# Sample scores as four 32-column products, sample values for two heads in turn, and the schedule repeated with latest times as ranks

## The chip, the cores and the metric

The kernel runs on one core of one Trainium2 chip. The metric is the device time of one execution in microseconds (us), from the start to the end of the program on that core, as a median of several runs. A profile of one execution shows the five engines: PE (TensorE, the matrix multiplier; its weight loads are listed apart as PEld), DVE (VectorE), ACT (ScalarE), POOL (GpSimd) and SP (SyncE, which here only issues transfers), and the DMA traffic. "Granted clock" is the share of full speed at which the throttle let TensorE run.

## The reference

One layer of a hybrid encoder. The input is a prompt of 2048 tokens and a "sample" of 8 sequences of 16 tokens (together 128 rows), each of width 1024. One input projection feeds three groups of heads: 6 forgetting-attention heads (FoX), 6 RWKV-7 heads and 4 heads that attend to 256 memory tokens. All heads are 64 wide. Their gated outputs go through one output projection and are added to the input. Cut to what the change touches, the sample's attention is:

```python
def fox_attend_block(q, cq, qpos, k, v, ck, kpos):
    s = jnp.einsum('bqhd,bkhd->bhqk', q, k, preferred_element_type=jnp.float32) * (HEAD_DIM ** -0.5)
    s = s + jnp.transpose(cq, (0, 2, 1))[..., :, None] - jnp.transpose(ck, (0, 2, 1))[..., None, :]
    mask = kpos[None, :] <= qpos[:, None]
    s = jnp.where(mask, s, jnp.finfo(jnp.float32).min)
    p = jax.nn.softmax(s, axis=-1)
    return jnp.einsum('bhqk,bkhd->bqhd', p.astype(v.dtype), v)

def fox_sample(q, k, v, logf, k_past, v_past, logf_past):
    keys = jnp.concatenate([k_past.astype(k.dtype), k], axis=1)      # 512 cached keys + 16 own, per sequence
    vals = jnp.concatenate([v_past.astype(v.dtype), v], axis=1)
    ...
def mem_attend(q_cols, mem_q_g, mk, mv):                             # the same without decay, 256 keys
    ...
```

Each of the 8 sequences has its own cached keys and values, so nothing is shared between sequences: a query row of sequence s may only meet the keys of sequence s.

## The kernel before, in words

**Two stages.** The first stage (lines 160 to 925) projects the input and runs the RWKV heads. The projection's products are named `pjd` and `pjt` (and `ptok`, `psh`); they stream 512 or 256 columns and depend on little. The RWKV work comes in blocks of 512 tokens for a pair of heads, twelve in all for the prompt. A block is a long chain of small products with work of the other engines between them: `gw`, `gx` (line 460 on), `pvt`/`pat`, `pmv`, `pbt` (turns and small triangular parts), `pz`, `pa`, `sc`, `sy` (the scan, eight dependent steps of `sc`), `yc`, `pss`, `spr` (the group norm). Small products use a quarter (64x64) or a sixteenth (32x32) of the array, so that several lie in it side by side. The second stage (line 926 on) does the attention and the output projection: for each key block `pm` (a running maximum over the keys), `pS` (scores, three products in the parts that a split number has), `P`, `Ph`, `Pl` (exponential on ACT, its split on ACT and POOL), `po` (values), and `py` (the output projection), which fills gaps.

**The sample** (function `sample`, lines 1189 to 1284) runs in the second stage, in five steps of two heads each: three FoX pairs with 512 keys and two memory pairs with 256. Per pair `load` brings the queries (`sC`), and then for each head in turn: `masked` takes a buffer `sD`, clears its first 640 columns on POOL (line 1219) and copies the queries into it (line 1222), and loads the cached values (`sA`, line 1226) and keys (`sB`, line 1229), 1 MB each for FoX and 0.5 MB each for memory. The 128 rows of the contraction hold the 64 dimensions of one sequence above those of another, so one product serves two sequences; the queries lie in a 128-column operand whose other columns are zero, and four such products (sequence pairs 0 to 3) add up in one bank `pS3` (the page shows it as `pS<-sB,sD`). `soft` is the softmax on DVE and ACT, with `pN` for the sample's own 16 keys. `turn` transposes the weights (`pt3b`). `values` multiplies them with `sA`: 8 sequences x 4 blocks of keys, each a product of a 64-column operand with 16 columns (`po<-sD,sA`), into the upper or lower half of the bank `po3` by head. A product in plain fp32 shows as two passes in the trace, so these 32 products are 64 passes.

**Buffers.** `sA`, `sB`, `sC`, `sD`, the output weights and some others share seven buffers of 8 KB per partition (`big`, line 965, `BIG` is 7), handed out in the order of the program.

**The order of the work.** The body of the kernel only records instructions. At the end `_arrange` (line 1849) sorts them anew for every engine: `_schedule` (line 1702) is a list scheduler with a model of each instruction's length, of TensorE's clock and of the buffers; at each step it takes the instruction that can start first, and among those that can start equally early the one with the smallest rank. A rank is the instruction's place in the recorded program, in time, less a weight times the longest chain that hangs on it. Four weights and two settings of a preference for staying in the array's present shape (`_WEIGHTS`, `_STAY`) are tried, and the order with the shortest modelled time is kept. SP's transfers are part of it and start in that order too: a transfer that waits for a buffer holds up those behind it.

Of the kernel before, what the change touches and what calls it, by code (L numbers as in the profile page):

```python
# [16 lines left out]
D = 1024  # L17
# [34 lines left out]
def kernel(ctx: ExitStack, tc: tile.TileContext, I: dict, O: dict):  # L52
# [24 lines left out]
    pools = _Pools(tc)  # L77
# [848 lines left out]
    with ExitStack() as p2:  # L926
# [261 lines left out]
        def sample(fox, hp):  # L1188
# [26 lines left out]
            def masked(h):  # L1215
                rr = slice(64 * h, 64 * h + 64)
                R["D"] = big("sD")
                qm = R["qm"] = R["D"][:, 0:640]
                G.memset(qm, 0.0)
# [11 lines left out]
            def soft(h):  # L1231
                hh, rr = 2 * hp + h, slice(64 * h, 64 * h + 64)
                pS = qb_.tile([128, 512], F32, tag="pm", name="pS3", bufs=PMB)
                for sp in range(4):
                    mm(pS[:, :nk], R["qm"][:, 128 * sp:128 * sp + 128], R["ck"][:, sp], start=sp == 0, stop=sp == 3)
                sb = R["sb"] = R["D"][:, 640:1280]
                st = wk.tile([128, 4], F32, tag="st3", name="st3")
                if fox:
# [3 lines left out]
                    dg = R["D"][:, 1920:2048]  # L1242
# [14 lines left out]
            def turn(h):  # L1257
                PT = R["PT"] = R["D"][:, 1280:1920].rearrange("p (a b) -> p a b", b=128)
# [194 lines left out]
_WEIGHTS = (0.0, 0.15, 0.3, 0.45)  # L1453
_STAY = (0, 2500)
# [247 lines left out]
def _schedule(prog, runs, over, weight, stay, loose=(), rank=None):  # L1702

    ins, eng, cost, deps, tiles, tile = prog
    nodes, node = runs
    count = len(nodes)
    of = [eng[m[0]] for m in nodes]
    before = [sorted({node[j] for k in m for j in deps[k]} - {x}) for x, m in enumerate(nodes)]  # L1710
    used = [sorted({n for k in m for n in tiles[k]}) for m in nodes]
    seen = lambda a, b: (0 if a == "PE" else 15) if a == b != "SP" else _SEEN[b]
    succ, soft, need = [[] for _ in nodes], [[] for _ in nodes], [len(d) for d in before]
    pool = {n: t.mls.memorylocations[0].ant_tile_pool_name for n, t in tile.items()}
    first, queue, uses, left, free_at = {}, {}, {}, {}, {}
    for x in range(count):
        for j in before[x]:
            succ[j].append(x)
        for n in used[x]:
            uses[n] = uses.get(n, 0) + 1  # L1720
            left[pool[n]] = left.get(pool[n], 0) + 1
            if n not in first:
                first[n] = x
                queue.setdefault(tile[n].tag, []).append(n)
                free_at[tile[n].tag] = [0] * tile[n].tag_meta.bufs
            elif first[n] not in before[x]:
                soft[first[n]].append(x)
                need[x] += 1
# [16 lines left out]
    for x in range(count - 1, -1, -1):  # L1745
# [3 lines left out]
        for q in after[x]:  # L1749
            gate[q] = max(gate.get(q, 0), below[x])  # L1750
# [222 lines left out]
```

## Time and profile before

| what | value |
|---|---|
| median of 3 runs | 1887.29 us (1883.79 to 1889.1) |
| time of the profiled execution | 1892.18 us |
| its span, first to last instruction | 1890.1 us |
| mean granted clock | 0.954 |
| PE busy | 1784.7 us (94%) |
| DVE, ACT, POOL busy | 949.0, 874.9, 788.9 us (50%, 46%, 42%) |
| sample's score products, FoX | 48 passes, 26.6 us busy |
| sample's value products | 512 passes, 34.4 us busy |
| read from and written to HBM | 211.47 and 87.12 MB |

"Busy" is the time in which at least one instruction of the engine was under way; matmuls overlap each other, so the time from one start to the next is shorter than the duration of one. In answers of the time line, a row is "start, length, engine, line, operation, out<-in, sizes of the operands, count"; a row of several passes runs from the first start to the last end. In answers by stretch ("windows"), each engine has its busy time and, in brackets, its number of instructions, then come the granted clock (PEclk), the share of DMA time and the GB/s. A pass that streams 512 columns shows 128x512, and 128*32 ahead of it would be the operand that stays in the array (rows x columns).

### The profile page before, as it was taken

The numbers are of one execution on the slowest core, as the hardware profiler recorded it, in microseconds if no ns is written. First come the engines' busy times: TensorE is split into PE (matmuls) and PEld (weight loads), VectorE is DVE, ScalarE is ACT, GpSimd is POOL, SyncE is SP. The second block draws the span as 40 slices with busy tenths as digits, with TensorE's granted clock in tenths as the row PEclk, the third lists the DMA queues.
The fourth block names the chain that finished last, engine by engine and source line by source line (L and its number), as shares of the span: only waits on it lengthen the run. The fifth ranks groups of instructions, "written<-read, shape, count | busy, mean of one in ns | idle before, by whom it ended". The sixth has DMA issues, their size and how long they took to land. (4 is left out here: it accounts for less than half of the span.)

```text
span 1890.1 us, 42104 instructions
## 1 busy us (share of the span) xinstructions
PE 1784.7 (94%) x16743; PEld 1426.4 (75%) x16743; DVE 949.0 (50%) x2330; ACT 874.9 (46%) x1727; POOL 788.9 (42%) x790
## 2 busy tenths in 40 slices
PE   5979999899999999998999997899898999999998
PEld 4878988688887888776788886666665666667776
DVE  6544444464444563453744543767445544386213
ACT  5424342424234323324232424687687555876452
POOL 5564342142132232121321331377485443866463
PEclk9989999999999999998999896799999889999999
DMA  7665455535436555354455344435546644254332
GB/s 245 228 227 169 153 175 182 191 123 176 163 117 207 177 167 196 109 176 163 127 164 188 103 155 123 141 126 167 188 137 209 186 139 137 67 179 145 137 114 100
DMA packets 213274, 301.34 MB, mean 159 GB/s; under 512 B 57444, under 2 KB 162454, under 8 KB 197206
## 3 DMA queue, kind: packets, MB, share of 16 engines
q1 hardware_dynamic: 213078, 298.66, 48.2%
q8 instruction: 131, 2.15, 0.5%
q14 instruction: 65, 0.53, 0.1%
HBM read 211.47 MB, written 87.12 MB: 158 GB/s over the span
## 5 line engine op out<-in xcount | busy, mean ns | idle before, releaser
L59 PE MATMUL pjd<-xk,w 128*128 128x512 f32 (+5 forms) x2280 | 526.4, 375 | 18.9 <-ACT qk L705 6.7
L59 PEld LDWEIGHTS pjd<-xk,w 128*128 128x128 f32 (+1 forms) x2280 | 385.8, 191 | 87.4 <-issue 9.5
L62 POOL TENSOR_TENSOR Pl<-P,Ph 128x512 fp32r<-128x512 f32 (+3 forms) x272 | 315.5, 1170 | 165.5 <-ACT Ph L1120 144.7
L59 PE MATMUL pjt<-w,xk 128*128 128x256 f32 x2040 | 290.3, 291 | 6.7 <-POOL w L62 4.2
L59 PEld LDWEIGHTS pjt<-w,xk 128*128 128x128 f32 x2040 | 266.2, 194 | 17.8 <-issue 5.0
L59 PE MATMUL py<-W,oh 128*128 128x512 f32 x816 | 247.1, 403 | 1.9 <-DVE rb L1162 0.9
L1117 ACT ACTIVATE P<-pS,NB 128x512 f32<-128x512 f32 x240 | 148.5, 623 | 110.9 <-PE pS L59 85.0
L59 PEld LDWEIGHTS py<-W,oh 128*128 128x128 f32 x816 | 150.9, 190 | 39.7 <-DVE rb L1162 1.4
L59 PE MATMUL pS<-Q,K 128*128 128x512 f32 (+2 forms) x480 | 160.1, 400 | 4.5 <-ACT P L1117 4.0
L59 PE MATMUL po<-Ph,vt 128*65 128x512 f32 x480 | 158.3, 381 | 0.3 <-ACT ob L1143 0.2
L1120 ACT CAST Ph<-P 128x512 fp32r<-128x512 f32 (+3 forms) x272 | 151.4, 564 | 9.2 <-PE po L59 4.0
L59 PEld LDWEIGHTS pS<-Q,K 128*128 128x128 f32 (+1 forms) x480 | 89.1, 198 | 36.6 <-ACT P L1117 16.0
L62 DVE TENSOR_TENSOR xo<-py,xo 128x512 f32<-128x512 f32 x68 | 46.8, 689 | 133.2 <-PE py L59 133.0
L1063 DVE CUSTOM_DVE_ANT_0 jk<-pm,nb,mx 128x512 bf16<-128x512 f32 (+3 forms) x144 | 93.0, 646 | 30.6 <-PE pm L59 22.8
L62 POOL TENSOR_TENSOR nr<-nr,mhalf 128x8 f32<-128x8 f32 (+2 forms) x43 | 61.5, 1431 | 97.5 <-DVE nr L68 73.0
L59 PE MATMUL pm<-K,Q 128*128 128x512 f32 (+2 forms) x240 | 96.4, 415 | 5.7 <-DVE mx L1063 4.8
L62 POOL TENSOR_TENSOR w<-wraw,w 128x1024 fp32r<-128x1024 f32 (+1 forms) x34 | 80.7, 2375 | 44.3 <-ACT w L197 43.2
L59 PE MATMUL po<-Pl,vt 128*65 128x512 f32 x240 | 91.1, 380 | 0.6 <-POOL Pl L62 0.6
L59 PEld LDWEIGHTS po<-Ph,vt 128*65 128x65 f32 x480 | 65.2, 141 | 26.6 <-issue 2.2
L705 ACT COPY qk<-pjt 128x512 f32<-128x512 f32 (+1 forms) x47 | 26.5, 563 | 113.1 <-PE pjt L59 92.0
L1063 DVE CUSTOM_DVE_ANT_0 jk<-pm,nb 128x512 bf16<-128x512 f32 (+3 forms) x96 | 61.3, 638 | 33.0 <-PE pm L59 28.3
L62 POOL TENSOR_TENSOR oh<-ot,oh 128x384 fp32r<-128x384 f32 (+2 forms) x38 | 45.2, 1191 | 57.0 <-ACT oh L1321 32.0
(392 smaller groups left out, 2942.6 us busy)
## 6 DMA issues: line engine op xcount, KB each, us to landing
w<-w_d SPq DMA_DIRECT2D x84, 1024.0 KB
w_d<-w SPq DMA_DIRECT2D x28, 1024.0 KB
y_d<-xo SPq DMA_DIRECT2D x21, 512.0 KB
wraw<-in_w_in SPq DMA_DIRECT2D x36, 256.0 KB
xo<-in_x SPq DMA_DIRECT2D x17, 512.0 KB
xo<-y_d SPq DMA_DIRECT2D x17, 512.0 KB
xt<-in_x SPq DMA_DIRECT2D x24, 256.0 KB
xraw<-in_xT SPq DMA_DIRECT2D x24, 256.0 KB
```

What stands on the lines that cost most here:

```text
L59: PE.matmul(out, lhsT, rhs, start=start, stop=stop, skip_group_check=True)
L62: e.tensor_tensor(out=out, in0=a, in1=b, op=op)
L705: S.copy(o_, out)
L1063: V.tensor_tensor_reduce(out=jk[:, :n], in0=pm[:, :n], in1=U["nb"][:, h, c0:c0 + n], scale=1.0, scalar=-3.0e38 if c0 == 0 else m_, op0=A_, ...
L1117: S.activation(P_[:, c0:], pS[:, c0:], AF.Exp, bias=NB[:, qb, 2 * hp + h, kt:kt + 1] if fox else 0.0)
L1120: S.copy(Ph[:, c0:], P_[:, c0:])
```

## The change

The change has three parts.

- **Scores.** The zero-padded operand shrinks from 640 to 128 columns, with the queries of sequence pair `sp` in columns 32sp to 32sp+31. The four products per head now have 32 columns each, go into four different 32-row strips of the bank, and no longer add up.
- **Values.** `values` is called once per pair instead of once per head, and issues the two heads' products in turn: upper half of the bank, lower half, upper half. The final scaling is one DVE instruction over 128 rows instead of two over 64. Both heads' `sD` and `sA` are now held until then.
- **The order.** `_schedule` also returns for each instruction the latest time at which it could start without making the modelled total longer. The planner runs five rounds from each of three weights (0.3, 0.45, 0.6); after each round the ranks move by 0.4 towards these latest times, and the shortest of the fifteen modelled orders is kept. The preference for staying in a shape is no longer tried.

```diff
             def masked(h):
                 rr = slice(64 * h, 64 * h + 64)
-                R["D"] = big("sD")
-                qm = R["qm"] = R["D"][:, 0:640]
+                D = R["D", h] = big("sD")
+                qm = R["qm"] = D[:, 0:128]
                 G.memset(qm, 0.0)
...
-                    V.tensor_copy(qm[64 * j:64 * j + 64].rearrange("p (s c) -> p s c", c=160)[:, :, 16 * j:16 * j + 16],
+                    V.tensor_copy(qm[64 * j:64 * j + 64].rearrange("p (s c) -> p s c", c=32)[:, :, 16 * j:16 * j + 16],
                                   q3[:, :, j, :])
                 m = big("sA")[:, 0:512 * nkt]
-                R["cv"] = m.rearrange("p (s t d) -> p s t d", t=nkt, d=64)
+                R["cv", h] = m.rearrange("p (s t d) -> p s t d", t=nkt, d=64)
...
                 for sp in range(4):
-                    mm(pS[:, :nk], R["qm"][:, 128 * sp:128 * sp + 128], R["ck"][:, sp], start=sp == 0, stop=sp == 3)
+                    mm(pS[32 * sp:32 * sp + 32, :nk], R["qm"][:, 32 * sp:32 * sp + 32], R["ck"][:, sp])
...
-            def values(h):
-                rr = slice(64 * h, 64 * h + 64)
+            def values():
                 po = qa.tile([128, 512], F32, tag="pt", bufs=PTB, name="po3")
+                rows = [slice(0, 64), slice(64, 128)]
                 if fox:
-                    mm(po[rr, 0:128], R["vn"][:, rr], R["PT"][:, 4, :], stop=False)
+                    for h, rr in enumerate(rows):
+                        mm(po[rr, 0:128], R["vn"][:, rr], R["PT", h][:, 4, :], stop=False)
                 for s_ in range(8):
                     for t in range(nkt):
-                        mm(po[rr, 16 * s_:16 * s_ + 16], R["cv"][:, s_, t, :], R["PT"][:, t, 16 * s_:16 * s_ + 16],
-                           start=not fox and t == 0, stop=t == nkt - 1)
-                stt(R["gt"][rr], po[rr, 0:128], 0.5, R["gt"][rr], M, M)
+                        for h, rr in enumerate(rows):
+                            mm(po[rr, 16 * s_:16 * s_ + 16], R["cv", h][:, s_, t, :], R["PT", h][:, t, 16 * s_:16 * s_ + 16],
+                               start=not fox and t == 0, stop=t == nkt - 1)
+                stt(R["gt"], po[:, 0:128], 0.5, R["gt"], M, M)
...
-                r += [lambda f=f, h=h: f(h) for f in (masked, soft, turn, values)]
-            return r + [out]
+                r += [lambda f=f, h=h: f(h) for f in (masked, soft, turn)]
+            return r + [values, out]
...
-_WEIGHTS = (0.0, 0.15, 0.3, 0.45)
-_STAY = (0, 2500)
+_TRIES = ((0.3, 0), (0.45, 0), (0.6, 0))
+_AGAIN = 5
+_SHIFT = 0.4
...
+    total = max(end)
+    late = [total - (end[x] - start[x]) for x in range(count)]
+    for x in reversed(order):
+        e = of[x]
+        for j in p.before[x]:
+            late[j] = min(late[j], late[x] - (1 if of[j] == e == "PE" else end[j] - start[j] + p.seen(of[j], e)))
+        for j, at in why[x]:
+            late[j] = min(late[j], late[x] - (at - start[j]))
+    return total, start, late
...
-    _, _, start = min((_schedule(prog, runs, over, w, stay, _LOOSE) for w in _WEIGHTS for stay in _STAY),
-                      key=lambda x: x[0])
+    found = []
+    for w, stay in _TRIES:
+        rank = p.emitted(w)
+        for _ in range(_AGAIN):
+            total, start, late = _schedule(p, rank, stay, _LOOSE)
+            rank = [(1 - _SHIFT) * a + _SHIFT * b for a, b in zip(rank, late)]
+            found.append((total, start))
+    _, start = min(found, key=lambda x: x[0])
```

The list `why` holds, for an instruction that took over a buffer, the instruction that had released it. The rest of the diff makes a class of what `_schedule` computed at its start.

The new order moves instructions everywhere. Three places follow. The first is PE in the last RWKV block of the first stage, the end of its chain; `pt<-ident,tok` are turns of keys for the second stage, `pjd` are products of the input projection. Before:

```order
L983 MATMUL pt<-ident,tok 128x128 x4
L59 MATMUL pmv<-su,gm 64x64 x16
L59 MATMUL pbt<-ident,bk 64x64 x32
L59 MATMUL pz<-su,XT_120 64x128 x16
L983 MATMUL pt<-ident,tok 128x128 x4
L59 MATMUL sc<-su,bt 64x64 x16
L59 MATMUL sy<-gm,su 64x64 x16
L59 MATMUL pa<-bt,za 64x64 x16
L59 MATMUL pa<-gm,za 64x64 x16
L983 MATMUL pt<-ident,tok 128x128 x6
L59 MATMUL sc<-ST,AD 128x64
L59 MATMUL sc<-st,AD 128x64 x3
```

Now, in the same place of that block:

```order
L59 MATMUL pbt<-ident,bk 64x64 x31
L59 MATMUL pjd<-xk,w 128x512 x6
L59 MATMUL pz<-su,XT_120 64x128 x16
L59 MATMUL pjd<-xk,w 128x512 x8
L59 MATMUL pa<-bt,za 64x64 x16
L59 MATMUL pa<-gm,za 64x64 x16
L59 MATMUL sc<-su,bt 64x64 x16
L59 MATMUL sy<-gm,su 64x64 x16
L59 MATMUL sc<-ST,AD 128x64
L59 MATMUL pjd<-xk,w 128x512 x3
L59 MATMUL sc<-st,AD 128x64
```

Before, the projection was finished ahead of this block, and 22 turns of keys stand in it; now 48 `pjt` and 39 `pjd` products of the projection stand between its steps, and the turns of keys come after it.

The second place is PE at the first sample pair (`pS_17445` and `pS_17630` are the scores of head 0 and head 1 of the pair before, `po_17500` the values of head 0). Before:

```order
L1263 MATMUL pt3b<-ident,sD 128x128
L59 MATMUL po_17500<-sD,sC 64x128
L59 MATMUL po_17500<-sD,sA 64x16 x32
L59 MATMUL pm<-K_16178,Q_17599 128x512
L59 MATMUL pS_17630<-sB,sD 128x512
L59 MATMUL pS<-Q_17197,K_16179 128x512 x2
L59 MATMUL pS_17630<-sB,sD 128x512
L59 MATMUL pS<-Q_17195,K_16177 128x512
L59 MATMUL pS<-Q_17197,K_16179 128x512
```

Now (`pS_17445` and `pS_17578` are the two heads' scores; the pair's values, `po_17668<-sD,sA 64x16 x64`, come 20 rows further on):

```order
L59 MATMUL pS_17445<-sB,sD 32x512 x4
L59 MATMUL pN_17452<-sC 128x128
L59 MATMUL pN_17452<-sD,one_82 128x128
L983 MATMUL pt<-ident,tok 128x128 x2
L59 MATMUL pm<-K_16177,Q_17563 128x512
L983 MATMUL pt<-ident,tok 128x128 x2
L1263 MATMUL pt3b<-ident,sD 128x128 x5
L59 MATMUL pS_17578<-sB,sD 32x512 x4
```

The second head's scores no longer wait behind the first head's values, and a head's four score products stand together, where attention products stood between them before.

The third place is SP, where the cached values and keys of a FoX pair are fetched. Before (the last FoX pair):

```order
L1226 DMA sA<-in_cfv 128x2048
L1229 DMA sB<-in_cfkT 128x2048
L1146 DMA sd<-rs 1x512
L1170 DMA rc<-sd 32x32
L1226 DMA sA<-in_cfv 128x2048
L1279 DMA o_d<-sC 128x128
L1173 DMA rd<-rc 32x32
L1176 DMA rb_18100<-rd 64x512 x2
L1229 DMA sB<-in_cfkT 128x2048
```

Now:

```order
L1226 DMA sA<-in_cfv 128x2048
L1281 DMA o_d<-sC 128x128
L1229 DMA sB<-in_cfkT 128x2048
L1226 DMA sA<-in_cfv 128x2048
L1146 DMA sd<-rs 1x512
L988 DMA vtok<-v_d 128x4x128
L1229 DMA sB<-in_cfkT 128x2048
```

The output of the pair before (`o_d<-sC`) now leaves between the first two of the four loads, so all four stand behind the values of the pair before; previously the first head's two loads stood ahead of them.

More of the change, by code (lines that the diff above doesn't have):

```diff
@@ L1699, in run @@
         return s, s + (own - c.own) + c.time + (w - 1) * c.own
[L1702 to L1728, printed above, removed]
-    after = [sorted({q for n in used[x] for q in over.get(pool[n], ())}) for x in range(count)]
-    pooled, below, at, own = {}, [0] * count, 0, [0] * count
-    def length(m, e):
-        c = [cost[k] for k in m]
@@ new lines, with __init__, seen, length @@
+class _Problem:
+    def __init__(self, prog, runs, over):
+        self.ins, self.eng, self.cost, deps, tiles, self.tile = prog
+        self.nodes, node = runs
+        nodes, tile = self.nodes, self.tile
+        self.count = count = len(nodes)
+        self.of = of = [self.eng[m[0]] for m in nodes]
+        self.before = before = [sorted({node[j] for k in m for j in deps[k]} - {x}) for x, m in enumerate(nodes)]
+        self.used = used = [sorted({n for k in m for n in tiles[k]}) for m in nodes]
+        self.succ, self.soft, self.need = [[] for _ in nodes], [[] for _ in nodes], [len(d) for d in before]
+        self.pool = pool = {n: t.mls.memorylocations[0].ant_tile_pool_name for n, t in tile.items()}
+        self.queue, self.uses, self.left, first = {}, {}, {}, {}
+        for x in range(count):
+            for j in before[x]:
+                self.succ[j].append(x)
+            for n in used[x]:
+                self.uses[n] = self.uses.get(n, 0) + 1
+                self.left[pool[n]] = self.left.get(pool[n], 0) + 1
+                if n not in first:
+                    first[n] = x
+                    self.queue.setdefault(tile[n].tag, []).append(n)
+                elif first[n] not in before[x]:
+                    self.soft[first[n]].append(x)
+                    self.need[x] += 1
+        self.after = [sorted({q for n in used[x] for q in over.get(pool[n], ())}) for x in range(count)]
+        self.spent = [self.length([self.cost[k] for k in m], e) for m, e in zip(nodes, of)]
+        self.below, gate = [0] * count, {}
+        for x in range(count - 1, -1, -1):
+            tail = 150 if of[x] == "PE" else 0
+            self.below[x] = self.spent[x] + max([self.below[s] + self.seen(of[x], of[s]) + tail for s in self.succ[x]] +
+                                                [gate.get(pool[n], 0) for n in used[x]], default=0)
+            for q in self.after[x]:
+                gate[q] = max(gate.get(q, 0), self.below[x])
+    @staticmethod
+    def seen(a, b):
+        return (0 if a == "PE" else 15) if a == b != "SP" else _SEEN[b]
+    @staticmethod
+    def length(c, e):
@@ L1741, in length, with emitted, _schedule @@
         return c[0].own
-    spent = [length(m, e) for m, e in zip(nodes, of)]
-    gate = {}
-    for x in range(count - 1, -1, -1):
-        tail = 150 if of[x] == "PE" else 0
-        below[x] = spent[x] + max([below[s] + seen(of[x], of[s]) + tail for s in succ[x]] +
-                                  [gate.get(pool[n], 0) for n in used[x]], default=0)
-        for q in after[x]:
-            gate[q] = max(gate.get(q, 0), below[x])
-    for x in range(count):
-        at += spent[x] if of[x] == "PE" else _STEP
-        own[x] = at - weight * below[x]
-    rank = rank or own
+    def emitted(self, weight):
+        at, rank = 0, []
+        for x in range(self.count):
+            at += self.spent[x] if self.of[x] == "PE" else _STEP
+            rank.append(at - weight * self.below[x])
+        return rank
+def _schedule(p, rank, stay, loose=()):
+    nodes, cost, of, used, tile, pool, count = p.nodes, p.cost, p.of, p.used, p.tile, p.pool, p.count
+    need, uses, left = list(p.need), dict(p.uses), dict(p.left)
+    queue = {t: list(q) for t, q in p.queue.items()}
+    free_at = {t: [(0, -1)] * tile[q[0]].tag_meta.bufs for t, q in queue.items()}
     free = dict.fromkeys(("PE", "DVE", "Activation", "Pool", "SP"), 0)
@@ L1801, in _schedule @@
         if not best:
-            return math.inf, order, start
+            return math.inf, start, start
         _, _, x, e, s, r = best
@@ L1806, in _schedule @@
         order.append(x)
+        for q in p.after[x]:
+            if q in pooled:
+                why[x].append((pooled[q][1], pooled[q][0]))
         for n in used[x]:
```

28 lines of the change are left out of this document (15 added, 13 removed).

## The prediction

> **What bounds the kernel now.** I read the page first, for which engine is full, then the answer by stretches, for where it is not, and the time line at the sample's products and at the switch from one array shape to another.
>
> ```profile
> span 1890.1 us, 42104 instructions
> PE 1784.7 (94%) x16743; PEld 1426.4 (75%) x16743; DVE 949.0 (50%) x2330; ACT 874.9 (46%) x1727; POOL 788.9 (42%) x790
> PE   5979999899999999998999997899898999999998
> PEclk9989999999999999998999896799999889999999
> ```
>
> PE is the only full engine, and the others have half of the time to spare. So the time is PE's work, plus PE's idle time, plus what the granted clock takes from it. The second and third of these sit in few places:
>
> ```profile
> core 0: us, PE busy (x) PEld busy (x) DVE busy (x) ACT busy (x) POOL busy (x), PEclk, DMA share, GB/s
> 0.00:144.40 144.40, 108.60 (x760) 98.67 (x760) 76.78 (x158) 59.58 (x121) 80.48 (x79) 0.92 0.72 233
> 325.40:362.70 37.30, 32.54 (x632) 24.54 (x631) 13.08 (x30) 16.27 (x39) 6.08 (x11) 0.91 0.60 212
> 849.30:889.20 39.90, 33.58 (x619) 27.71 (x619) 13.87 (x33) 16.92 (x40) 6.19 (x12) 0.79 0.50 175
> 981.50:1015.60 34.10, 34.02 (x747) 31.27 (x747) 13.52 (x27) 12.30 (x27) 10.41 (x11) 1.00 0.29 97
> 1133.50:1181.20 47.70, 38.02 (x630) 30.59 (x630) 18.12 (x45) 23.16 (x48) 8.65 (x12) 0.63 0.41 122
> 1440.00:1640.00 200.00, 187.70 (x1189) 131.33 (x1188) 100.87 (x289) 118.19 (x230) 96.15 (x95) 0.90 0.48 152
> 1640.00:1890.10 250.10, 240.67 (x1135) 175.91 (x1134) 110.28 (x235) 139.56 (x249) 141.22 (x125) 1.00 0.38 130
> ```
>
> Columns: stretch, its length, busy time of each engine with its number of instructions, granted clock. Call a stretch's loss its length less PE busy times clock. The rows from 325.4, 849.3, 981.5 and 1133.5 are the chains of the third, ninth, tenth and last RWKV block of the prompt. The losses are 37.3 - 32.54 x 0.91 = 7.7, 39.9 - 33.58 x 0.79 = 13.4, 0.1 and 47.7 - 38.02 x 0.63 = 23.7 us. The tenth block has 119 projection products between its steps and loses nothing; the last has none. The sample stands from 1440 to 1640, where PE is busy 187.7 of 200 us at a clock of 0.90.
>
> **The change part by part. Scores.** Time line rows at the sample:
>
> ```profile
> 1566.09 3.60 PE L59 MATMUL pS<-sB,sD 128*128 128x512 f32 x8
> 1512.76 1.02 PE L59 MATMUL pS<-sB,sD 128*128 128x512 f32 x2
> 1624.04 0.60 PE L59 MATMUL pS<-sB,sD 128*128 128x256 f32 x2
> 543.49 1.10 PE L59 MATMUL gr<-AR,bk 64*64 64x128 f32 x32
> 561.14 1.09 PE L59 MATMUL spr<-ident,inv 128*64 128x128 f32 x16
> L59 PE MATMUL po<-sD,sA 128*64 128x16 f32 x512 | 34.4, 216 | 0.5 <-ACT sD L1264 0.5
> ```
>
> A FoX head's four products are 8 passes in 3.60 us. A memory head streams half as much, 1.8 us. Six and four heads: 28.8 us. Side by side, four products should last as long as one, which is two passes: 1.02 us, and 0.60 with 256 columns; six and four of these are 8.5 us. That saves 20.3 us of PE time at full clock. No row of this trace has four 32-column operands over all 128 rows in the array. The nearest are `spr`, two 64-column halves, and `gr`, four 64x64 quarters, each streaming 128 columns a pass. A last pass runs out for some 0.22 us (the last row's 216 ns). So `spr` starts a pass every (1.09 - 0.22) / 15 = 58 ns and `gr` every (1.10 - 0.22) / 31 = 28 ns; the full-width scores need (3.60 - 1.02) / 6 = 430 ns for 512 columns, 107 ns for 128. One, two and four operands thus stream at one, two and four times the speed. But in `gr` a partition is read for two operands at a time, here for four. If no more than two streams can be read at once, each head needs twice the streaming: 1.02 + 0.86 and half of that, together 15.3 us, and 13.5 are saved. I take 20, the row of side-by-side operands being nearest, and keep 13 as the other end.
>
> **Values.** The rows, and the nearest one for two column halves in turn:
>
> ```profile
> 1493.56 3.85 PE L59 MATMUL po<-sD,sA 128*64 128x16 f32 x64
> 1625.60 2.04 PE L59 MATMUL po<-sD,sA 128*64 128x16 f32 x32
> 607.91 1.15 PE L59 MATMUL sc<-su,bt 128*64 128x64 f32 x32
> 586.31 0.75 PE L59 MATMUL gw<-x,gm 32*32 32x32 f32 x64
> ```
>
> One head is 64 passes in 3.85 us, 58 ns from start to start ((3.85 - 0.22) / 63): all go to the same half of the array. `sc` has the same 128x64 operands, but in turn in both halves: (1.15 - 0.22) / 31 = 30 ns, although it streams 64 columns and not 16. So a FoX pair's 128 passes take about 128 x 0.030 + 0.2 = 4.0 us and a memory pair's 2.1, three and two of them 16.3 us, against 6 x 3.85 + 4 x 2.04 = 31.3 us: 15 us saved. [...]
>
> **Clock.** After a burst of values the clock often drops, though PE was never idle:
>
> ```profile
> 1493.30:1497.40 4.10, 4.10 (x68) 4.07 (x68) 0.57 (x4) 1.79 (x4) 1.11 (x1) 1.00 0.03 6
> 1497.40:1501.00 3.60, 3.60 (x11) 2.00 (x11) 3.07 (x6) 0.92 (x2) 3.03 (x4) 0.57 0.70 207
> 1564.70:1568.10 3.40, 3.40 (x14) 2.03 (x15) 1.48 (x5) 1.89 (x3) 1.14 (x2) 1.00 0.53 155
> 1528.20:1531.60 3.40, 3.40 (x13) 2.66 (x13) 0.80 (x4) 2.82 (x6) 0.93 (x1) 0.56 0.68 212
> 1531.60:1535.00 3.40, 3.32 (x10) 1.86 (x9) 2.61 (x8) 3.33 (x7) 2.02 (x3) 0.50 0.96 405
> ```
>
> The bursts that end at 1497.4 and 1528.2 cost 1.5 and 3.2 us; the one that ends at 1564.7 cost nothing. With half as many bursts, each twice as dense, I take 3 us back, between 0 and 6. [...]
>
> **Switches of shape.** What the array pays to change between shapes, and the length of the projection's passes:
>
> ```profile
> 1133.14 0.48 PE L59 MATMUL pjd<-xk,w 128*128 128x512 f32 x1
> 1133.55 0.75 PE L59 MATMUL gw<-x,gm 32*32 32x32 f32 x64
> 1111.75 3.94 PE L59 MATMUL pjt<-w,xm 128*128 128x256 f32 x32
> 1124.56 7.67 PE L59 MATMUL pjd<-xk,w 128*128 128x512 f32 x33
> L1219 POOL MEMSET sD<- x10: 630/632/689, 1415.8 to 1600.3; 128x640 f32 x10
> ```
>
> A `pjd` pass takes 0.23 us (7.67 / 33), a `pjt` pass 0.12 (3.94 / 32). From the last `pjd` to the first `gw` pass 0.41 us, so the switch costs 0.18. In PE's new order the shape changes 1175 times, before 1146: 29 x 0.18 = 5 us more. The smaller clearing on POOL and the single scaling on DVE lie beside PE's other work and give nothing; if that cover were gone, ten clearings of a fifth of 0.63 us would be a gain of 5 us.
>
> Sum of the sample: 20 + 15 + 3 - 5 = 33 us of PE time. From 1440 on PE is busy 428 of 450 us, and ACT, the next, at 57%, so nine tenths of it should reach the end: **30 us**, with ends at 15 (two streams, no clock, most of the saving met by waits) and 40.
>
> **The order.** In the last RWKV block 48 `pjt` and 39 `pjd` now stand where none stood: 5.9 + 9.0 = 14.9 us of work leaves the time ahead of the chain and goes into its 23.7 us of loss. In the ninth block the `pjd` grow from 40 to 73: 7.7 us into 13.4. In the third they grow from 48 to 123, 17 us, of which I count 5, since only 7.7 are lost there. The first two blocks give these up (285 to 140 and 184 to 120 products), and keep more than the tenth has. Against it, 22 key turns of 128 columns, some 0.11 us each, leave the last chain and come after it: about 3 us. Together 24.6; I take **22 us**, because some blocks that gave up filling may show a gap. The start (144.4 - 108.6 x 0.92 = 44.5 us lost, much of it the first loads) and all of the attention are reordered too, with nothing in the order that tells me the sign; I allow 15 us both ways. The end of the program, some 79 `py` products after the last sums, is as it was.
>
> Sum: 1892.2 us of the profiled execution, less 52, is 1840. The runs' median lies 4.9 us below that execution, so the forecast is **1835 us**.
>
> **The rivals.** *Two streams.* The four score products share their reading, so that 13 us are saved instead of 20; nine tenths of the difference is 6: 1841 us. For it speaks that no row shows more than two operands read from a partition at once. [...]
>
> *The order gives its gain back.* The planner's times are a model; if an RWKV step comes later than planned, PE, which takes its instructions in order, waits where before it had other work. Then only the sample's 30 us stay: 1857 us. For it: the old order came from the same model and left 23.7 us in one chain. Against it: the covered chain from 981.5 to 1015.6 lost 0.1 us.
>
> *The change doesn't do what it says*: products of 32 columns run one after the other, value products don't overlap, and the new order is no better. 1887 us.
>
> *Slower: the sample's loads.* Both heads' `sD` and `sA` are held until the pair's values, so five of the seven buffers come free at one moment, and the next pair's loads wait for it on SP, with the attention's small transfers (`md`, `Q`, `rb`, `nb`) behind them. SP knew this wait before:
>
> ```profile
> SPq L1226 <- PE po L59: 42.9, 7, 12.0
> ```
>
> PE would then wait for the first scores. After the first pair's values 74 attention products stand before the next pair's scores, some 15 us; the first head's 2 MB landed within 7 us in the rows from 1528.2 to 1535 (3.4 us at 212 and 3.4 at 405 GB/s). So this decides the sign only if the loads come about 10 us later than their cover at each of five pairs and the clock halves after it: 5 x 12 = 60 us against the 52, which gives about 1895 us. That would take 2 MB in 25 us, less than 80 GB/s.
>
> **How the numbers follow.** Forecast 0.55, two streams 0.15, order given back 0.16, nothing done 0.06, slower by the loads 0.08. The low end is all of the sample (40) and all loss of the three chains (45) and 10 at the start: 1892 - 95, less the 4.9, is about 1795. The high end is the sample's low end with no gain of the order, 1892 - 15 - 5 = 1872. That leaves out the last two rivals, 0.14, and a little below. A measurement here can tell 0.3%, 5.7 us, from no change. All cases but the last two are faster by more: 0.86; the same 0.06; slower 0.08.
>
> **What would show it.** Right: a FoX head's scores as 8 passes in about 1 us, a pair's values as 128 passes in about 4, the last RWKV chain with a clock near 1 and a PE that hardly idles, and the sample's stretch shorter by some 30 us. Wrong, step by step: score passes at 1.9 us (two streams) or 3.6 (none); values at 58 ns a pass; a chain of 47 us as before; PE waiting for `sB` ahead of scores. The forecast falls as a whole if the start or the attention loses more than 50 us that they did not lose before.

## The result, and the profile after

The changed kernel takes 1831.5 us (1829.6 to 1832.3 in 4 runs), the kernel before 1888.2 us beside it. The ratio is 0.9699, with a 95% interval from 0.9683 to 0.9714. The forecast was 1835 us. The total was right; most of this part is on why the terms that it was added up from were not.

The page of the profile after, its first line, the line of engines and the two lines of 40 slices:

```profile
span 1830.5 us, 42049 instructions
PE 1718.1 (94%) x16743; PEld 1370.1 (75%) x16743; DVE 934.0 (51%) x2325; ACT 872.3 (48%) x1727; POOL 782.4 (43%) x790
PE   4989999999999999999999998799899898999998
PEclk9999999999999999999999998799999898999999
```

PE is busy for 67 us less and as full as before (94%). The drops of the clock in slices 3, 19 and 23, all in stage 1, are gone. The weak slices 25 and 26 (the end of stage 1 and the start of attention) and 32 to 34 (the sample) remain.

The operations that the change touches, from the time line (start, length) and from the groups (busy, mean ns):

```profile
1456.45 1.06 PE L59 MATMUL pS<-sB,sD 128*32 128x512 f32 x8
1531.96 0.64 PE L59 MATMUL pS<-sB,sD 128*32 128x256 f32 x8
1440.12 3.86 PE L59 MATMUL po<-sD,sA 128*64 128x16 f32 x128
L59 PE MATMUL po<-sD,sA 128*64 128x16 f32 x512 | 17.2, 216 | 0.5 <-ACT sD L1264 0.5
```

A FoX head's scores are 8 passes in 1.06 us (3.60 before), and a pair's values 128 passes in 3.86 us. Four operands stream side by side: 1.06 to 1.07 us in four of the six FoX heads, at a granted clock of 1.00, where one 128-column product alone took 1.02 before. The other two heads took 1.94 us, at 0.50. The values' busy time is halved (34.4 to 17.2).

For the time, I cut each run at two landmarks. The first is the centring product `yc` of the last RWKV chain, where stage 1 ends. The second is ACT's first copy of an attention result (L1140), where the first unit of attention ends. Between them lies the boundary. Rows by stretch (start:end, length, busy time of each engine, granted clock), before and after:

```profile
0.00:1171.70 1171.70, 1100.77 (x13227) 942.60 (x13227) 582.24 (x1460) 422.87 (x881) 381.11 (x414) 0.96 0.52 169
1171.70:1214.60 42.90, 37.07 (x159) 23.98 (x160) 29.87 (x79) 22.12 (x45) 14.64 (x17) 0.66 0.39 119
1214.60:1890.10 675.50, 646.90 (x3359) 459.80 (x3357) 336.92 (x793) 429.94 (x802) 393.15 (x359) 0.97 0.44 145
```

```profile
0.00:1121.90 1121.90, 1068.50 (x13196) 916.34 (x13196) 554.62 (x1443) 410.26 (x857) 374.76 (x407) 0.98 0.53 172
1121.90:1178.50 56.60, 38.94 (x190) 26.51 (x190) 38.18 (x91) 32.77 (x67) 17.27 (x25) 0.70 0.58 182
1178.50:1830.50 652.00, 610.70 (x3361) 427.25 (x3359) 341.16 (x792) 429.24 (x804) 390.39 (x359) 0.97 0.45 150
319.00:356.30 37.30, 33.79 (x609) 26.21 (x609) 15.77 (x32) 19.72 (x44) 8.07 (x13) 0.91 0.61 207
830.70:870.60 39.90, 39.90 (x689) 30.25 (x689) 20.14 (x47) 22.23 (x50) 8.61 (x13) 1.00 0.61 201
1085.50:1125.00 39.50, 37.57 (x673) 31.71 (x673) 7.77 (x20) 12.44 (x27) 3.19 (x4) 0.91 0.28 93
```

Stage 1 is 49.8 us shorter, the boundary 13.7 us longer, the rest 23.5 us shorter. The last three rows are the chains of the third, ninth and last RWKV block: the ninth lost 13.4 us and now loses nothing, the last lost 23.7 and now loses 39.5 - 37.57 x 0.91 = 5.3, the third hardly moved (7.7 to 6.6).

The clock in a long row is rounded to two places, which is worth up to 5.5 us either way in stage 1. So for what follows I added up windows of 5 us: *idle* is length less PE's busy time, *clock* is busy time x (1 - granted clock), *work* is busy time x clock. Stage 1 before: idle 70.9, clock 42.0, work 1058.8. After: 53.4, 15.1, 1053.4. More than half of the gain there (27 of 50) is clock.

### The profile page after: what moved, and what is told of

It is laid out like the page before. It is cut to its first block, busy times and chain, and to the rows that moved or that the text cites. A ratio compares the mean times of both kernels' runs of the same rounds, so it can differ in the third digit from the quotient of the medians.

```text
span 1830.5 us, 42049 instructions
## 1 busy us (share of the span) xinstructions
PE 1718.1 (94%) x16743; PEld 1370.1 (75%) x16743; DVE 934.0 (51%) x2325; ACT 872.3 (48%) x1727; POOL 782.4 (43%) x790
## 5 line engine op out<-in xcount | busy, mean ns | idle before, releaser
L59 PE MATMUL pjd<-xk,w 128*128 128x512 f32 (+4 forms) x2280 | 520.1, 373 | 14.6 <-DVE xk L62 6.7
L59 PEld LDWEIGHTS pjd<-xk,w 128*128 128x128 f32 (+1 forms) x2280 | 381.9, 190 | 79.1 <-issue 10.8
L59 PE MATMUL py<-W,oh 128*128 128x512 f32 x816 | 236.2, 402 | 2.3 <-DVE rb L1162 1.6
L59 PEld LDWEIGHTS py<-W,oh 128*128 128x128 f32 x816 | 150.5, 190 | 38.3 <-DVE rb L1162 2.1
L59 PE MATMUL pS<-Q,K 128*128 128x512 f32 (+2 forms) x480 | 155.5, 392 | 8.3 <-ACT P L1117 8.0
L59 PE MATMUL po<-Ph,vt 128*65 128x512 f32 x480 | 151.3, 373 | 1.2 <-ACT ob L1143 0.7
L59 PEld LDWEIGHTS pS<-Q,K 128*128 128x128 f32 (+1 forms) x480 | 87.4, 195 | 40.5 <-ACT P L1117 24.7
L59 PE MATMUL pm<-K,Q 128*128 128x512 f32 (+2 forms) x240 | 95.8, 411 | 19.5 <-DVE Q L62 13.1
L59 PEld LDWEIGHTS pm<-K,Q 128*128 128x128 f32 x240 | 47.1, 198 | 44.7 <-DVE mx L1063 18.2
L62 POOL TENSOR_TENSOR oh<-ot,oh 128x384 fp32r<-128x384 f32 (+2 forms) x38 | 44.9, 1183 | 74.3 <-ACT oh L1323 39.5
```

The costliest lines, as they stand in the source:

```text
L59: PE.matmul(out, lhsT, rhs, start=start, stop=stop, skip_group_check=True)
L62: e.tensor_tensor(out=out, in0=a, in1=b, op=op)
```

## The experiments

All runs in one table, by the landmarks; idle, clock and work are those of the rest, from the first unit of attention to the end. The profiled execution is one of several runs, so its total can stand some us from the median. The rows come from several chips; the last column is the ratio to the kernel before on the same chip, with its 95% interval.

| kernel | median us | stage 1 | boundary | rest | idle | clock | work | ratio |
|---|---|---|---|---|---|---|---|---|
| before | 1888.2 | 1171.7 | 42.9 | 675.5 | 28.6 | 19.9 | 627.0 | |
| after | 1831.5 | 1121.9 | 56.6 | 652.0 | 41.3 | 14.9 | 595.8 | 0.9699 (0.9683 to 0.9714) |
| after, again | 1829.6 | 1117.0 | 56.0 | 657.3 | 35.6 | 27.4 | 594.3 | 0.9682 (0.9658 to 0.9706) |
| order only | 1838.0 | 1123.1 | 55.2 | 658.6 | 22.8 | 9.5 | 626.2 | 0.9708 (0.9668 to 0.9747) |
| order only, again | 1836.5 | 1111.8 | 56.8 | 658.9 | 21.6 | 12.4 | 624.9 | 0.9715 (0.9692 to 0.9737) |
| products only | 1871.5 | 1169.0 | 41.7 | 659.6 | 44.8 | 15.9 | 598.8 | 0.9913 (0.9882 to 0.9944) |
| after, wide scores | 1842.8 | 1117.8 | 55.9 | 670.9 | 38.3 | 17.7 | 614.9 | 0.9741 (0.9712 to 0.9770) |
| after, heads apart | 1858.4 | 1122.4 | 54.9 | 681.2 | 39.3 | 34.1 | 607.8 | 0.9821 (0.9782 to 0.9859) |
| projection first | 1836.5 | 1140.2 | 42.3 | 653.1 | 41.2 | 16.1 | 595.8 | 0.9720 (0.9683 to 0.9757) |
| heavy plan | 1842.8 | 1115.4 | 55.1 | 663.9 | 48.4 | 16.3 | 599.2 | 0.9759 (0.9732 to 0.9786) |
| other search | 1850.1 | 1148.5 | 54.9 | 642.2 | 33.2 | 13.9 | 595.1 | 0.9799 (0.9771 to 0.9827) |
| values twice | 1849.0 | 1114.7 | 55.0 | 675.3 | 39.1 | 24.7 | 611.5 | 0.9785 (0.9756 to 0.9814) |
| two halves | 1828.0 | 1116.8 | 54.2 | 650.0 | 36.0 | 13.1 | 600.9 | 0.9676 (0.9647 to 0.9705) |
| order only, light scores | 1837.9 | 1116.9 | 54.9 | 663.6 | 24.9 | 19.3 | 619.4 | 0.9738 (0.9714 to 0.9762) |

My theory after the result: two gains that add, some 29 us from the sample's products and the rest from the order. The rivals: the order is everything, or neither pays without the other.

**Order only and products only.** The first takes the new planner with the functions `masked`, `soft`, `turn` and `values` of before; the second takes these as changed, with the planner of before:

```diff
-            def values():
+            def values(h):
...
-_TRIES = ((0.3, 0), (0.45, 0), (0.6, 0))
-_AGAIN = 5
-_SHIFT = 0.4
+_WEIGHTS = (0.0, 0.15, 0.3, 0.45)
+_STAY = (0, 2500)
```

(The first two lines are of the one, the others of the other.)

> Only the new planner; the sample's scores and values as before (accumulating 128-column products, one head after the other). The first 2300 lines of PE's order are those of the changed kernel, so stage 1 should end about 50 us earlier than before, at about 1122. Theory, two gains that add: the sample's shorter products are worth 29 us of the 57, the order the rest; about 1860 us (1852 to 1868). Rival A, the order is everything and the PE time saved in the sample would have been idle: 1832 to 1840. Rival B, the order pays only with the lighter sample, since what it frees early is waited out later: 1878 or more.

> Only the new products; the planner of before. PE's order is that of before up to the attention before the sample, so stage 1 should be unchanged (end near 1171.6). Theory, two gains that add: sample's stretch 29 us shorter, nothing else; about 1859 us (1852 to 1868). Rival A, PE time freed in the sample turns into waits for ACT and DVE unless the order is new too: 1875 or more. Rival B, the products alone are nearly everything: 1840 or less.

Measured: 1838.0 and 1836.5 us for the order alone, 1871.5 for the products alone. My theory falls. The order alone brings 52 to 54 us of the 57, and the products alone 16 to 19 (0.9913, whose interval is 11 to 22 us); together they should bring some 70 and bring 57. Rows from the first unit to the end, of the order alone and of the products alone:

```profile
1178.30:1836.90 658.60, 635.80 (x3361) 451.64 (x3359) 341.02 (x797) 428.07 (x804) 393.60 (x359) 0.98 0.44 149
```

```profile
1210.70:1870.30 659.60, 614.78 (x3359) 428.20 (x3357) 336.56 (x788) 428.25 (x801) 389.04 (x359) 0.97 0.45 148
```

Both take 16 to 17 us out of this stretch, by different ways. The order keeps PE's work and takes out idle time and lowered clock (48.5 to 32.3 us in the table). The products take out 28 us of work, and 12 come back as idle time and clock. The change has 30 us less work than the order alone, and 24 of them come back (29 between the second profiles of the two). Most of it can be placed: where one unit of attention follows another, the new unit's row maxima go to DRAM and return as `Q<-md` (this load is issued at 1539.57 and 1430.41 us, late in the two stretches below), and its scores read them: the first of their products over 65 rows, which take them in, start at 1543.10 and 1444.67 us. The two stretches, with light products and with the order alone:

```profile
1527.50:1551.50 24.00, 16.91 (x125) 10.85 (x126) 8.41 (x29) 11.13 (x24) 6.59 (x9) 0.72 0.83 254
1419.50:1431.50 12.00, 8.47 (x32) 3.89 (x32) 5.89 (x14) 7.74 (x18) 3.29 (x6) 0.50 0.47 137
```

```profile
1530.80:1554.80 24.00, 23.71 (x155) 16.84 (x153) 3.71 (x12) 16.57 (x35) 13.71 (x14) 0.93 0.49 152
1422.80:1434.80 12.00, 11.06 (x58) 5.89 (x57) 8.88 (x25) 7.38 (x14) 2.89 (x4) 1.00 0.42 118
```

The light products lose 24 - 16.91 x 0.72 = 11.8 and 12 - 8.47 x 0.50 = 7.8 us; the heavy ones, in the order that was planned for them, 1.9 and 0.9. These two places hold 17 of the 24 us. What PE stands at there is mostly the sample itself: the turn of its weights (`pt3b`) waits for the sample's softmax on DVE (line L68). Its waits (us, times, longest) with light products, in the first stretch, in the second, and from 1380 to 1660 us:

```profile
PE pt3b L1263 <- DVE sD L68: 4.1, 2, 2.1
PE pt3b L1263 <- DVE sD L68: 3.1, 1, 3.1
PE pt3b L1263 <- DVE sD L68: 8.3, 6, 3.1
```

The order alone has no such wait from 1380 to 1660 in its first profile and 0.3 us in its second; the products alone have 6.2. So the rival that let the freed time turn into waits for other engines holds in part, and in the new order too.

**Wide scores and heads apart.** Each undoes one half of the products, and the order of every engine is kept. In the first the planner is given the light products' costs; in the second the order within a pair's values is changed after planning.

```diff
-                    mm(pS[32 * sp:32 * sp + 32, :nk], R["qm"][:, 32 * sp:32 * sp + 32], R["ck"][:, sp])
+                    mm(pS[:, :nk], R["qm"][:, 128 * sp:128 * sp + 128], R["ck"][:, sp], start=sp == 0, stop=sp == 3)
...
-            at[prog[0][k].name] = (start[x], j)
+            late = o is not None and o.tensor.name.startswith("po3") and o.offset >= 64 * 512
+            at[prog[0][k].name] = (start[x], j + 1000 * late)
```

> The changed kernel, each engine's order kept as it is (POOL clears 640 columns where it cleared 128), the sample's score products alone again 128 columns wide and accumulating. PE does 20 us more (8.5 to 28.8). Theory, PE time on the path counts at nine tenths: 18 us slower than the changed kernel, about 1850 (1844 to 1854). Rival, the sample waits for DVE's softmax, so the longer products hide in the 22 us of PE's idle time there: 1832 to 1838.

> The changed kernel, each engine's order kept, only within each pair's 64 value products (and the two of the new tokens) those of head 0 first and then those of head 1, not in turn. PE does 15 us more (16.3 to 31.3). Theory, PE time on the path counts at nine tenths: 14 us slower than the changed kernel, about 1845 (1841 to 1848). Rival 1, the cost is hidden in PE's idle time: 1832 to 1836. Rival 2, the gain of the values came from one wait and one eviction for two heads, not from the two halves of the array running at once: no change.

Measured: 1842.8 and 1858.4. The first falls between the two ranges that were given, the second above all three. By the ratios the wide scores cost 8 to 11 us and the heads apart 23 to 26. The rows of the scores' groups with wide scores:

```profile
L59 PE MATMUL pS<-sB,sD 128*128 128x512 f32 x48 | 27.2, 721 | 0.0
L59 PE MATMUL pS<-sB,sD 128*128 128x256 f32 x32 | 9.2, 441 | 0.0
```

Work rises by 19 to 21 us (595.8 and 594.3 to 614.9), as the prediction's 20.3 had it, and idle time hardly falls. So in a fixed order the products stand on the path, though not at nine tenths: by the ratios about half of the work reaches the end, and in this profile (of an execution of 1846.4 us, 3.6 above the median) the rest of the program is 14 to 19 us longer. This is no contradiction to the first pair of runs: there the planner had laid heavy products where PE had nothing else, as the two stretches above show.

The heads apart cost more than their work, which rose by only 12 to 14 us. Here the clock moved too: with each pair's values as one half of the array and then the other, it stood at 0.62 to 0.70 in the bursts and at 0.50 behind. In all three bursts of the FoX pairs the first 3.7 to 4 us ran at 0.84 to 1.00 and the rest at 0.50. Two of them, each with the 3 us behind it:

```profile
1438.50:1449.80 11.30, 11.30 (x133) 11.26 (x131) 0.95 (x4) 0.00 (x0) 0.11 (x1) 0.62 0.01 3
1449.80:1452.80 3.00, 3.00 (x9) 2.02 (x9) 0.87 (x4) 0.55 (x1) 0.10 (x1) 0.50 0.73 205
1533.60:1544.50 10.90, 10.90 (x133) 10.86 (x130) 0.71 (x3) 1.30 (x2) 3.24 (x4) 0.65 0.15 50
1544.50:1547.50 3.00, 3.00 (x10) 2.09 (x11) 2.10 (x7) 1.15 (x3) 0.40 (x2) 0.50 0.71 184
```

**Values twice.** Is it the length of the burst or the half-empty array? Here each pair's products, heads in turn, are issued twice, in the same place of the same order:

```diff
+                for again in (False, True):
...
-                stt(R["gt"], po[:, 0:128], 0.5, R["gt"], M, M)
+                stt(R["gt"], po[:, 0:128], 0.25, R["gt"], M, M)
```

> The changed kernel with the same order, only each pair's value products (64 and the two of the new tokens, the heads in turn) are issued a second time straight behind the first, and their sum is halved again on DVE. It adds about as many PE microseconds as taking the heads one after the other did (16), but with both halves of the array at work all the time. If a burst's length drops the clock, the bursts of nearly 8 us should show a granted clock near 0.5 in the microseconds behind each, as with the heads apart, and the time be about 1858 (1850 to 1866). If it is the half-empty array that drops the clock, the clock stays near 1 behind them and the time is about 1846 (1842 to 1849).

This kernel doesn't give the reference's result, so it stands here for its time alone. Measured: 1849.0 us. The three bursts of the FoX pairs, each with the 3 us behind it:

```profile
1430.80:1438.60 7.80, 7.80 (x265) 7.77 (x262) 0.95 (x4) 0.00 (x0) 0.00 (x0) 1.00 0.03 6
1438.60:1441.60 3.00, 3.00 (x20) 2.37 (x20) 1.63 (x6) 1.59 (x3) 0.21 (x1) 1.00 0.68 180
1474.30:1485.40 11.10, 11.10 (x265) 11.06 (x261) 0.97 (x3) 0.41 (x1) 2.02 (x3) 0.67 0.22 66
1485.40:1488.40 3.00, 3.00 (x10) 2.33 (x9) 1.20 (x4) 1.99 (x4) 0.20 (x1) 0.50 0.64 158
1524.20:1532.00 7.80, 7.80 (x265) 7.77 (x261) 0.74 (x4) 1.30 (x2) 3.13 (x3) 1.00 0.22 71
1532.00:1535.00 3.00, 3.00 (x20) 2.14 (x18) 2.63 (x7) 2.08 (x5) 1.05 (x2) 1.00 0.62 172
```

Two of the three bursts of 7.8 us keep the clock at 1.00, and the time lies at the upper edge of what the half-empty array gave. So length alone doesn't drop the clock; with half of the array at work all three FoX bursts dropped it. But two halves at work don't keep it either. The second burst falls here too, as it does in the changed kernel, and in the changed kernel's second profile the clock is low behind all three bursts of about 4 us, heads in turn:

```profile
1439.10:1442.10 3.00, 3.00 (x9) 2.02 (x9) 0.87 (x4) 0.57 (x1) 0.21 (x1) 0.50 0.68 164
1481.90:1484.90 3.00, 3.00 (x9) 2.18 (x10) 1.54 (x5) 2.34 (x4) 0.52 (x2) 0.55 0.80 203
1523.90:1526.90 3.00, 3.00 (x13) 2.13 (x11) 2.10 (x7) 1.15 (x3) 0.50 (x2) 0.55 0.60 149
```

Over the profiles in the table, the clock is under 0.7 in the 3 us behind 8 of 24 FoX bursts with the heads in turn and issued once (eight profiles), behind 15 of 24 bursts of a single head (four profiles), and behind 3 of 3 with the heads apart. A half-empty array goes with more frequent drops; what sets one off stays open.

**Projection first.** The boundary is 13.7 us longer. SP's first key load there, in the time line before and after, with the waits (engine, line, releaser; us, times, longest) of PE in the boundary before and after, and of the load after:

```profile
1133.65 0.38 SPq L980 DMA_DIRECT2D tok<-k_d  x1
PE pm L59 <- DVE Q L62: 0.6, 1, 0.6
```

```profile
1125.87 0.36 SPq L980 DMA_DIRECT2D tok<-k_d  x1
SPq L980 <- PE pjd L59: 16.4, 1, 16.4
PE pm L59 <- DVE Q L62: 12.7, 4, 5.4
```

Before, the load went out as the last chain began (1133.55). After, it went out 4 us behind the chain's end, when the last projection product was done, and PE then waited 12.7 us, in four waits, for the split queries. The experiment ranks the projection's last products earlier and schedules once more:

```diff
+    early = [name(m).startswith("pj") and s > 1030000 for m, s in zip(p.nodes, start)]
+    _, start, _ = _schedule(p, [s - 30000 * e for s, e in zip(start, early)], 0, _LOOSE)
```

> The changed kernel, but the projection's products that its order places in the last part of stage 1 are ranked 30 us earlier, so that they no longer fill the last RWKV chain. PE's order is unchanged in its first 1796 rows. Theory of the trade: the projection's operands and accumulators lie where stage 2's turned keys lie, so whoever covers the last chain with projection pays at the boundary. Stage 1 should end 10 to 20 us later (1132 to 1142), the boundary should fall from 56 us to about 43, and the total stay within about 8 us of the changed kernel, 1828 to 1840. Rival, the long boundary comes from how attention's preparation itself is ordered now: the boundary stays at 52 or more and the total is 1843 or more.

```profile
1108.52 0.36 SPq L980 DMA_DIRECT2D tok<-k_d  x1
```

```profile
0.00:1140.20 1140.20, 1078.35 (x13226) 924.28 (x13226) 566.24 (x1459) 423.24 (x880) 377.93 (x414) 0.98 0.53 174
1140.20:1182.50 42.30, 35.21 (x163) 23.38 (x164) 31.56 (x79) 21.53 (x44) 12.68 (x17) 0.76 0.38 121
```

The load goes out during the chain again, and PE's wait for the split queries is gone; stage 1 is 18.3 us longer and the boundary 14.3 us shorter. The total is 1836.5 us (1825 to 1842), the same within the intervals. So the trade is shown for this kernel: covering the last chain with projection gives most of its gain back at the boundary.

**Heavy plan, other search, two halves.** These ask whether a better order for the light products is there. The first plans with the costs of the heavy products (in the third round from the weight 0.6), the second searches from another weight, the third joins the changed kernel's stage 1 to ranks from the other search's stage 2:

```diff
+        if o.startswith("pS3"):
+            c.shape, c.load, c.own = (128, 128), 2 * 128 / 2.4, 2 * max(128, c.n) / 1.2 + 10
...
-_TRIES = ((0.3, 0), (0.45, 0), (0.6, 0))
-_AGAIN = 5
-_SHIFT = 0.4
+_TRIES = ((0.55, 0),)
+_AGAIN = 3
+_SHIFT = 0.5
...
+    _, start, _ = _schedule(p, [b if l else a for a, b, l in zip(first, second, later)], 0, _LOOSE)
```

> The changed kernel's light products, in the order that the planner finds when it is told that the scores and values cost what they cost before (one product of the array at a time). Stage 1's order is unchanged. Theory A, a matter of order: the order with the heavy products lost only 20 us of PE time from the sample to the end where the light ones lose 47, so the planner's order for light products is poor and this one wins some 15 us or more: 1805 to 1817. Theory B, no matter of order: the heavy products were themselves what filled PE's gaps where one unit of attention follows another, so light products leave those gaps empty in any order: 1826 to 1840.

> The changed kernel, planned in one search from the weight 0.55 with half a step to the latest times and three rounds. Every order that the planner finds this way differs in stage 1 as well as later. If the repeated rounds converge on what bounds the kernel, any good search gives about the same time: 1826 to 1838. If a round is one draw among many and the choice of the best draw did the work, this one can be off by 10 us or more either way.

> Stage 1 in the order of the changed kernel, stage 2 ranked by the order that the other search found. That order needed 642 us from the end of the first unit of attention to the end, the changed kernel's 652. If what an order wins in stage 2 does not depend on how stage 1 was ordered, about 1822 (1815 to 1828). If the ranks find another order once the stage begins in another state, 1828 or more.

> The changed kernel once more, for comparison on the same chip and in the same rounds: 1826 to 1838, and stage 1's end in its profile between 1115 and 1125, as in four builds that share its order there.

Measured: 1842.8, 1850.1, 1828.0 and 1829.6 us. The heavy plan with light products is worse than both theories gave: its rest idles 48.4 us, 4.0 of it in one wait for a load of keys (`sB`). So an order planned with heavy costs doesn't suit light products. The other search shows that a better order of the rest exists:

```profile
1203.40:1845.60 642.20, 609.08 (x3357) 425.67 (x3355) 340.20 (x791) 427.33 (x806) 388.18 (x359) 0.97 0.46 153
```

With the same work as the changed kernel (595.1) its rest is 10 to 15 us shorter; but its stage 1 is 27 to 32 us longer (idle 70.7 us there, clock 23.7), so this search did not come to the same bound, and its result looks like one draw among many. To join the two good halves brought 0.9676 against 0.9682 on the same chip, no difference: begun from another state, the ranks gave another order, with 650.0 us for the rest. No version that beats the changed kernel came out of this.

**Order only, light scores.** The order alone, kept on every engine, with light scores in it, and the order alone once more beside it:

```diff
-                    mm(pS[:, :nk], R["qm"][:, 128 * sp:128 * sp + 128], R["ck"][:, sp], start=sp == 0, stop=sp == 3)
+                    mm(pS[32 * sp:32 * sp + 32, :nk], R["qm"][:, 32 * sp:32 * sp + 32], R["ck"][:, sp])
...
+            score = outs[0].tensor.name.startswith("pS3")
+            cols = 128 if score else cols
```

> The new planner with the sample as before (the order of the run that changed the order only, kept on every engine), and in that order the score products alone made light: 32 columns each, side by side where they follow each other. PE does 15 to 19 us less (some of the four products have transposes or other products between them there). Theory A, PE time on the path counts at nine tenths in this order too, as it did in the changed kernel's order: 14 to 17 us faster than the order alone, about 1822 (1818 to 1828). Theory B, in an order planned for heavy products, these are what fills PE while one unit of attention follows another: PE's idle time and lowered clock grow instead, and the time is within 7 us of the order alone, 1831 to 1842.

> The order alone once more, on the same chip and in the same rounds: 1834 to 1842.

Measured: 1837.9 against 1836.5. Nothing is gained, as theory B had it, but not only for its reason:

```profile
1458.21 1.05 PE L59 MATMUL pS<-sB,sD 128*32 128x512 f32 x2
L59 PE MATMUL pS<-sB,sD 128*32 128x512 f32 x48 | 15.4, 662 | 0.3 <-DVE mx L1063 0.3
L59 PE MATMUL pS<-sB,sD 128*32 128x256 f32 x32 | 7.5, 391 | 0.0
```

Here full-width products stand between the four of a head in three of the six FoX heads and in all memory heads, and a lone light product (2 passes) takes 1.05 us, as a wide one does (1.02). The scores are busy 22.9 us, not the 10.7 that they take in the changed kernel; the work of the rest fell by only 6 us and its lowered clock took 7 more. So this run doesn't test the theories with the 15 to 19 us that it was meant to take out. What it shows is that light products pay where they stand together. The planner takes up to 64 successive products of one small shape as one piece (`_visits`); products entered as full-width, as here, are placed one by one. In the heavy plan the pieces were made before the costs were raised, and all ten heads' scores stayed together there.

## Why the prediction was right, and where it was not

- **Scores, 20 us of PE time**: right. 19 to 21 us of work by the wide scores, 1.06 us a head at a granted clock of 1.00. The rival of two streams is dead: it needed 1.9 us at that clock. (Its sum comes to 15.0 us, not 15.3, and the low end of the range to 1792, not 1795; nothing hangs on either.)
- **Values, 15 us**: right in size; 12 to 14 us of work by the heads apart, and 17.2 us less busy time.
- **Clock, 3 us back**: not to be seen. The lowered clock took 19.9 us of the rest before, and 14.9 and 27.4 in two profiles of the changed kernel, which is 5 less or 7.5 more. Against the heads apart in the same order (34.1) it is 7 to 19 us.
- **Switches of shape, 5 us more**: no run takes them by themselves, so the term is not shown.
- **The sample's sum of 33 us of PE time**: right; work from the first unit on fell from 627.0 to 595.8, 31 us.
- **"Nine tenths of it should reach the end: 30 us"**: this step failed. It was argued from a stretch where PE is busy 428 of 450 us. With the planner of before the products brought 16 to 19 us, and with the new order 5 to 8 by the medians and 0.1 to 0.3 per cent by the ratios, which the intervals don't tell from nothing. A PE that is 95% busy over a stretch can still have its free time at the few places where the removed work was the filling, here mostly the sample's own softmax and the change from one unit of attention to the next. In a fixed order each half of the products, undone, costs 8 to 26 us; the planner, which lays heavy products into gaps, is what makes them cheap.
- **The order, 22 us**: mis-sized. The order alone brings 52 to 54: stage 1 49 to 60 in the two profiles, the boundary 12 to 14 the other way, and some 17 from the attention on, to which the prediction gave 15 with no sign. In windows of 4 us, idle and clock together from block to block of stage 1: the ninth 17.4 to 1.4 (the prediction counted 7.7), the last 18.9 to 4.9 (14.9 counted), the third 9.4 to 8.4 (5 counted), the fifth and eleventh 9.7 to 0.1 (not counted), the start 43.9 to 40.7. The first block, which gave up filling, went the other way, 2.0 to 6.3. So the filling that moved in did not merely replace its own length; where a stall went, the lowered clock behind it went as well.
- **Against it, "about 3 us" for the key turns behind the last chain**: failed. Not their 22 transposes count but the wait that opens: the keys' load is behind the last projection product, and the splits on ACT and DVE that lay under the chain now stand bare. 13.7 us, and the run with the projection first shows that it is the price of covering the last chain.
- **The rival of the sample's loads**: it did not come. From 1400 to 1600 us SP's wait for a pair's values is shorter than before (42.9), and none of PE's waits there is for a load of the sample:

```profile
SPq L1226 <- PE po L59: 9.3, 4, 4.7
```

That the forecast of 52 us and the result of 57 agree is luck: the sample was set too high and the order too low by about the same. The rival in which the order gives its gain back was the wrong way round: what was given back was the products'. The 40 us between the products alone and the change come from the repeated rounds with latest times: with one round, the new weights give the order of the products alone on every engine, row for row.

## What to carry to other kernels

Cost an edit on the busiest engine twice: once in the fixed order, once in the order that a planner finds for the old work; here the saving that reached the end lay near the second. When filling is moved into a stall, count the lowered clock behind the stall as well (27 of the 50 us that stage 1 won here), and look at whose buffers the filling keeps occupied: here the next stage's first load waited 16.4 us for the last projection product. Products that can run side by side saved time here only where nothing full-width stood between them (scores busy for 10.7 us standing together, 22.9 us where most were parted), so the order and the products have to be made for each other.

## What the runs showed of the hardware

- Four products with 128x32 operands, each reading another operand over all 128 partitions, stream fully side by side: 8 passes of 512 columns in 1.06 us in the changed kernel, against 1.05 us for 2 passes of one alone in the order alone with light scores, both at a granted clock of 1.00.
- A PE that is busy without a gap can lose its clock. With 128x64 operands and 16 columns on one half of the array after the other, it fell to 0.50 some 3 to 4 us into all three bursts and stayed there behind them. With both halves in turn, bursts of 7.8 us kept 1.00 in two cases of three, but single bursts of 3.9 us were followed by less than 0.7 in 8 cases of 24; so a full array goes with fewer drops here and doesn't rule them out.
- The same order of instructions in stage 1 ended between 1111.8 and 1123.1 us in ten profiles of eight builds. The changed kernel's own two profiles were 4.9 us apart, with 15.1 and 7.7 us taken by the lowered clock. Differences of that size in one profile are no result.
